# Projections beside the forgetting attention: staged in two alternating sets of tiles, stored from POOL's queue

## The chip, the cores and the metric

The kernel runs on one core of one Trainium2 chip. The metric is the device time of one execution in microseconds (us). Before the change it was 2829.44 us, the median of three runs (2826.55 to 2829.99). The engines are PE (matrix multiply; PEld is its weight load), DVE (vector), ACT (scalar and activation), POOL (GpSimd) and SP (SyncE, which here only issues DMAs). Every engine works through its own instructions in a fixed order.

## The reference

The program is two transformer blocks on 1024 tokens of width 1024. The first (a hybrid of attention and convolution, and a mixture of experts) is not touched. The second has a recurrent branch (HGRN, 8 heads) and a forgetting attention ("fox", 16 heads of 64), followed by an output projection. What matters here is the second branch and the projections that feed it:

```python
u = rmsnorm_2(h, norm_w[i])
proj = jnp.einsum('bsd,de->bse', u, w_in[i])
hq, hf, hi, hg, fq, fk, fv, fg, fz = jnp.split(proj, SPLIT_POINTS, axis=-1)
y_h = hgrn2_branch(hq, hf, hi, lb_all[i], hgrn_gn[i]) * jax.nn.silu(hg)
y_f = fox_branch(fq, fk, fv, fz, fox_fb[i]) * jax.nn.silu(fg)
...
# fox_branch, one block of 128 queries
logits = (jnp.einsum('bhtd,bhsd->bhts', qb, kb).astype(f32) * scale
          + F[:, :, q0:q1, None] - F[:, :, None, :q1])
probs = jax.nn.softmax(jnp.where(mask, logits, -jnp.inf), axis=-1)
outs.append(jnp.einsum('bhts,bhsd->bhtd', probs.astype(v.dtype), vb))
```

## The kernel before

All products are made from numbers that are split into a high and a low part (three matrix products for one). `u` stays in SBUF as `uh`, `ul`. A **job** is one block of weight columns (`wk` loads it into `raw`, ACT writes `whi`, DVE writes `wlo`), and a job has several **units**; one unit makes a 128x512 piece of the projection in PSUM (`mm`) with 24 matrix products of 512 columns, or 48 of 256.

`fox_jobs(pr)` lists the jobs for a pair of heads. There are three kinds of unit: `value` (V, for every second pair, four units), `qk` (Q and K, two units each) and `gate` (two units). A unit of the first two kinds calls `staged`: ACT writes the high part into the tile `sth`, DVE writes the low part into `stl`, and both are stored to DRAM tensors (`V2_d`, `Q2_d`, `K2_d`). A `gate` unit works in `sth` alone (four ACT and two DVE instructions) and stores to `G2_d`. The profile drops the digit and shows these tensors as V_d, Q_d, K_d, G_d. Both tiles lie in the pool `pj` with `SB = 1`, that is one buffer each: the next unit's ACT write to `sth` waits until the store of the unit before it has landed, and its DVE write to `stl` likewise. The stores are issued by SP (lines 1166, 1173, 1181), two DMAs for each part of V, one for the others: 144 DMAs in all, 128 to 256 KB each. SP also issues all loads of this stage, in one order with the stores: the weights (`raw`, line 835) and, for each head, `K`, `Q`, `V`, `nF` and for each pair `gs` (lines 1268 to 1280).

The units of pair 0 (ten of them) run inside the last HGRN head, the other 54 beside the attention. `fox()` goes over 128 steps (16 heads by 8 query blocks). `fox_scores` runs two steps ahead: PE makes `sc`, DVE makes `lg` (from `nF` and the tile `Gd`), ACT takes the exponential. `fox_values` transposes `lg` on PE (`tp`), ACT and DVE split it into `pT`, and PE multiplies it with V (`av`). Units are due at one in about 1.93 steps (`FPROJ / left` = 104 / 54). After step 104 come the weights and first parts of the output projection (`out_load`, `out_part`).

POOL's queue holds in this stage: `Gd` (line 1277, once a head), the clearing of `pT` (1318), and the stores of `yT_d` (line 76, from `self.store`). The final order on each engine is set by a scheduler that simulates the program, not by the text alone.

Of the kernel before, what the change touches and what calls it, by code (L numbers as in the profile page):

```python
# [8 lines left out]
F32 = mybir.dt.float32  # L9
F32R = mybir.dt.float32r  # L10
# [9 lines left out]
P = 128  # L20
# [7 lines left out]
EPS = 1e-6  # L28
NE = 16
CAP = 128  # L30
SB = 1
LOOK = 1
NCV = 31
NR = 6
# [6 lines left out]
def f(ap):  # L41
    return ap.bitcast(F32)
# [7 lines left out]
class Kernel:  # L50
# [729 lines left out]
    def block2(self):  # L780
        with ExitStack() as st:
            self.stu = ExitStack()
            up = self.pool(self.stu, "uT", side="right")
            self.u = [(self.t(up, [P, KB, 512], F32R, f"uh{g}"), self.t(up, [P, KB, 512], F32R, f"ul{g}")) for g in range(2)]
            self.pj = self.pool(st, "pj")
            self.jobs, self.ready = [], []
            with ExitStack() as st2:
                self.pp = self.pool(st2, "b2p", 2, space=PSUM)
                self.ffn_out()
                self.hgrn()  # L790
            self.fox()
# [353 lines left out]

    def fox_jobs(self, pr):

        nc, w = self.nc, self.pj

        def staged(ps, scale=None):  # L1150
            hi = self.t(w, [P, 512], F32R, "sth", bufs=SB)
            lo = self.t(w, [P, 512], F32R, "stl", bufs=SB)
            if scale is None:
                self.split(ps, hi, lo)
            else:
                nc.scalar.activation(hi, ps, AF.Copy, scale=scale)
                nc.vector.scalar_tensor_tensor(lo, ps, scale, f(hi), op0=ALU.mult, op1=ALU.subtract)
            return hi, lo

        def value(b):  # L1160
            def go(ws):
                ps = self.toks(ws, b)
                parts = staged(ps.rearrange("p b c -> p (b c)"))
                for j, part in enumerate(parts):
                    for k in range(2):
                        nc.sync.dma_start(self.V2_d[j, (b + k) * P:(b + k + 1) * P, pr * P:pr * P + 256], f(part[:, k * 256:(k + 1) * 256]))
            return go

        def qk(dst, scale, g):
            def go(ws):  # L1170
                parts = staged(self.chan(ws, g), scale)
                for j, part in enumerate(parts):
                    nc.sync.dma_start(dst[pr, j, :, g * 512:(g + 1) * 512], f(part))
            return go

        def gate(g):
            def go(ws):
                ps = self.chan(ws, g)
                e = self.sigmoid(w, ps, "sth", SB)
                nc.vector.tensor_tensor(e, e, ps, op=ALU.mult)  # L1180
                nc.sync.dma_start(self.G2_d[pr, :, g * 512:(g + 1) * 512], e)
            return go
        if pr % 2 == 0:
            self.job(6144 + pr * P, 256, [value(b) for b in range(0, 8, 2)])
        self.job(4096 + pr * P, P, [qk(self.Q2_d, -0.125, g) for g in range(2)])
        self.job(5120 + pr * P, P, [qk(self.K2_d, None, g) for g in range(2)])
        self.job(7168 + pr * P, P, [gate(g) for g in range(2)])

    def fox(self):
        nc, I = self.nc, self.I  # L1190
        with ExitStack() as st:
            w = self.w = self.pool(st, "fx")
            pp = self.pp = self.pool(st, "fxp", 2, space=PSUM)
            self.nmm = 2
            self.cmask = self.t(w, [P, P], F32, "cmask")
            nc.sync.dma_start(self.cmask, I["k_cmask"])
            for pr in range(1, 8):
                self.fox_jobs(pr)
            units = [(h, tb) for h in range(16) for tb in range(8)]
            left = len(self.ready) + sum(len(j[2]) for j in self.jobs)  # L1200
            due = [((j - 3) * FPROJ / left, self.fill) for j in range(left)]
            due += [(x, lambda q=q: self.out_load(q)) for q, x in enumerate(FLOAD)]
            due += [(FK0 + j * (len(units) - FK0) / 8, lambda j=j: self.out_part(0, j)) for j in range(8)]
            due.sort(key=lambda x: x[0])
            self.X = {}
            LOOK = self.LOOK
            for i in range(LOOK):
                self.fox_scores(*units[i])
            for i, u in enumerate(units):
                if i + LOOK < len(units):  # L1210
                    self.fox_scores(*units[i + LOOK])
                while due and due[0][0] <= i:
                    due.pop(0)[1]()
                self.fox_values(*u)
            for tb in range(2):
                self.out_part(1, tb)
# [15 lines left out]
    def out_part(self, half, tb):  # L1232

        nc, w = self.nc, self.pj
        t = slice(tb * P, (tb + 1) * P)
        y = self.y_half(w, half, tb, ("raw", "whi", "wlo"), (2, 3))
        h = self.t(w, [P, 512], F32, "sth", bufs=SB)
        nc.sync.dma_start(h, self.h2_d[t, 0:512])
        ps = self.t(self.pp, [P, 512], F32, "mm", bufs=self.nmm)
        wo = [self.wo[0, half * 2 + q] for q in range(2)]  # L1240
        self.mm3(ps, [(y[k], (wo[k // 4][0][:, k % 4, :], wo[k // 4][1][:, k % 4, :])) for k in range(KB)])
        nc.vector.tensor_tensor(h, h, ps, op=ALU.add)
        self.store(self.h2_d[t, 0:512], h)
# [291 lines left out]
```

## Time and profile before

| | |
|---|---|
| median of 3 runs | 2829.44 us |
| the profiled execution | 2830.79 us |
| its span, first to last instruction | 2828.9 us |
| PE busy | 2636.2 us, 93% |
| last HGRN stage, 1390 to 1890 us | PE busy 498.46 of 500 us |
| attention with projections, 1890 to 2450 us | PE busy 523.12 of 560 us |

The profile covers one execution. Its span leaves 1.9 us outside, and the execution is 1.35 us over the median. Times in the rows are counted from the span's start. A "busy" PE is one that has a matrix product under way; the granted clock (PEclk) is 1.00 at 2.4 GHz and 0.50 at 1.2 GHz.

### The profile page before, as it was taken

What the parts mean: (1) busy time and instruction counts of PE and PEld (TensorE: products, weight loads), DVE (VectorE), ACT (ScalarE), POOL (GpSimd) and SP (SyncE); (2) the same over time, 40 slices, a digit from 0 to 9 for tenths busy, and PEclk for the clock granted to TensorE, in tenths of its full rate; (3) what the DMA queues carried; (4) which work ended last, traced back from release to release, by engine and by line L of the source; (5) the groups of instructions that cost most, each with busy time, mean ns of one, the idle gap of its engine ahead of it and who ended that gap; (6) DMA issues with size and microseconds to landing.
All of it is one profiled execution on the core that took longest, in us unless ns stands there. A gap on an engine that the chain in (4) does not pass through costs nothing.

```text
span 2828.9 us, 38725 instructions
## 1 busy us (share of the span) xinstructions
PE 2636.2 (93%) x14237; PEld 2216.2 (78%) x14237; DVE 1998.8 (71%) x3298; ACT 1620.6 (57%) x2858; POOL 250.1 (9%) x355
## 2 busy tenths in 40 slices
PE   8999999898799999997799999998999998989998
PEld 5777888787588877775689999997878787777786
DVE  6965899845698888885656767763777676785535
ACT  4213898734477777775644555543665665674335
POOL 0101000001300000000100000000111110231000
PEclk9999999999899999999799999999999999999999
DMA  7666332245699999997512122336665667465612
GB/s 302 203 236 211 90 96 90 91 160 198 241 390 381 363 377 370 375 359 239 218 39 46 46 46 38 49 79 171 168 168 136 161 156 144 143 186 200 195 60 82
DMA packets 306018, 516.44 MB, mean 183 GB/s; under 512 B 52529, under 2 KB 180094, under 8 KB 304804
## 3 DMA queue, kind: packets, MB, share of 16 engines
q1 hardware_dynamic: 288556, 456.04, 51.0%
q0 software_dynamic: 11136, 36.25, 4.3%
q10 hardware_dynamic: 6136, 21.67, 2.0%
q8 instruction: 113, 1.85, 0.3%
q14 instruction: 77, 0.63, 0.1%
HBM read 421.01 MB, written 92.88 MB: 182 GB/s over the span
## 4 chain that ended last, share of the span: by engine, by line
PE 72%; DMA 10%; ACT 7%; DVE 6%; issue 3%; SPq 1%; POOL 0%; DVEq 0%; ACTq 0%; POOLq 0%
PE mm L82 13%; PE mm L84 13%; PE mm L83 12%; PE av L1333 2%; PE pu L763 2%; PE pu L764 2%; PE pu L762 2%; PE pg L763 2%; PE py L764 2%; PE py L763 2%; PE py L762 2%; PE pg L764 2%; PE sc L1052 2%; PE pg L762 2%; PE tp L1324 1%
## 5 line engine op out<-in xcount | busy, mean ns | idle before, releaser
L88 DVE TENSOR_TENSOR wlo<-raw,whi 128x2048 fp32r<-128x2048 f32 (+1 forms) x280 | 541.9, 1962 | 172.2 <-ACT whi L87 168.1
L87 ACT CAST whi<-raw 128x2048 fp32r<-128x2048 f32 (+1 forms) x284 | 459.8, 1656 | 136.5 <-PE mm L83 62.1
L82 PE MATMUL mm<-uh,whi 128*128 128x512 f32 x640 | 257.4, 402 | 0.9 <-ACT uh L824 0.9
L83 PE MATMUL mm<-ul,whi 128*128 128x512 f32 x640 | 254.1, 397 | 0.0
L84 PE MATMUL mm<-uh,wlo 128*128 128x512 f32 x640 | 253.8, 397 | 0.0
L84 PE MATMUL mm<-whi,ul 128*128 128x256 f32 x768 | 220.9, 288 | 0.0
L82 PE MATMUL mm<-whi,uh 128*128 128x256 f32 x768 | 220.6, 287 | 0.0
L83 PE MATMUL mm<-wlo,uh 128*128 128x256 f32 x768 | 218.2, 284 | 0.0
L82 PEld LDWEIGHTS mm<-whi,uh 128*128 128x128 f32 x768 | 147.4, 192 | 0.2
L84 PEld LDWEIGHTS mm<-whi,ul 128*128 128x128 f32 x768 | 147.5, 192 | 0.1
L83 PEld LDWEIGHTS mm<-wlo,uh 128*128 128x128 f32 x768 | 147.2, 192 | 0.2
L1302 ACT ACTIVATE lg<-lg,sm 128x128 f32<-128x128 f32 (+7 forms) x128 | 99.5, 777 | 82.2 <-DVE sm L1301 81.6
L84 PEld LDWEIGHTS mm<-uh,wlo 128*128 128x128 f32 x640 | 122.3, 191 | 24.4
L446 ACT ACTIVATE e<-sc,mx 128x512 f32<-128x512 f32 (+1 forms) x192 | 117.9, 624 | 40.3 <-DVE mx L445 39.5
L82 PEld LDWEIGHTS mm<-uh,whi 128*128 128x128 f32 x640 | 122.2, 191 | 22.9 <-ACT uh L824 1.4
L83 PEld LDWEIGHTS mm<-ul,whi 128*128 128x128 f32 x640 | 122.4, 191 | 21.7
L82 PE MATMUL mm<-xh,whi 128*128 128x512 f32 x320 | 127.2, 399 | 2.4 <-DVE stl L88 1.4
L1333 PE MATMUL av<-pT,V 128*128 128x256 f32 x640 | 109.9, 300 | 19.6 <-ACT pT L87 13.8
L83 PE MATMUL mm<-xl,whi 128*128 128x512 f32 x320 | 126.9, 398 | 0.0
L84 PE MATMUL mm<-xh,wlo 128*128 128x512 f32 x320 | 126.3, 396 | 0.5 <-DVE wlo L88 0.5
L1333 PEld LDWEIGHTS av<-pT,V 128*128 128x128 f32 x640 | 92.3, 196 | 43.0 <-ACT pT L87 30.5
L1298 DVE SCALAR_TENSOR_TENSOR lg<-sc,FT,nF 128x512 f32<-128x512 f32 (+3 forms) x160 | 91.6, 582 | 39.7 <-PE sc L1295 27.1
(392 smaller groups left out, 7006.2 us busy)
## 6 DMA issues: line engine op xcount, KB each, us to landing
raw<-in_w_gate_dram SPq DMA_DIRECT2D x64, 1024.0 KB
raw<-in_w_up_dram SPq DMA_DIRECT2D x64, 1024.0 KB
raw<-in_w_down_dram SPq DMA_DIRECT2D x64, 1024.0 KB
raw<-in_w_in_dram SPq DMA_DIRECT2D x76, 512.0 KB
wada<-in_w_ada_dram SPq DMA_DIRECT2D x32, 512.0 KB
Q<-Q_d SPq DMA_DIRECT2D x64, 256.0 KB
yraw<-yT_d SPq DMA_DIRECT2D x22, 512.0 KB
wa<-in_w_ada_dram SPq DMA_DIRECT2D x8, 1024.0 KB
```

Source lines behind the costliest of these rows:

```text
L82: self.nc.tensor.matmul(ps, ah, bh, start=(i == 0), stop=False)
L83: self.nc.tensor.matmul(ps, ah, bl, start=False, stop=False)
L84: self.nc.tensor.matmul(ps, al, bh, start=False, stop=(i == n - 1))
L87: self.nc.scalar.copy(hi, src)
L88: (eng or self.nc.vector).tensor_tensor(lo, src, f(hi), op=ALU.subtract)
L446: nc.scalar.activation(e[:, c0:c0 + n], ps[:, :n], AF.Exp, scale=-1.0, bias=mx[:, m, c:c + 1], accum_out=sm[:, m, c:c + 1])
L762: self.nc.tensor.matmul(ps[n], xh[:, i, :], hi[:, k, c], start=(i == 0), stop=False)
L763: self.nc.tensor.matmul(ps[n], xh[:, i, :], lo[:, k, c], start=False, stop=False)
L764: self.nc.tensor.matmul(ps[n], xl[:, i, :], hi[:, k, c], start=False, stop=(i == KB - 1))
L1298: nc.vector.scalar_tensor_tensor(lg[:, c0:c0 + full], ps[:, :full], Ft, nF[:, c0:c0 + full], op0=ALU.subtract, op1=ALU.add)
L1302: nc.scalar.activation(lg[:, :n], lg[:, :n], AF.Exp, scale=-1.0, bias=sm[:, 0:1], accum_out=sm[:, 1:2])
L1333: nc.tensor.matmul(ps[:, :256], V[:, k, :], pT[k // 4][j][:, k % 4, :], start=(k + j == 0), stop=(k == nkb - 1 and j == 1))
```

## The change

Inside `fox()`, a second set of `sth` and `stl` is made in the pool `fx`, and units take the two sets in turn. During the last HGRN head there is still only the set in `pj`. All 144 stores go through `self.store`, that is through POOL's queue in place of SP's. `SB` is gone; the tiles that used it keep one buffer in their pool. `out_part` keeps its `sth` in `pj`.

```diff
@@ class Kernel, block2
             self.jobs, self.ready = [], []
+            self.staging, self.turn = [self.pj], 0
...
@@ fox_jobs
-        nc, w = self.nc, self.pj
+        nc = self.nc
+
+        def place():
+
+            self.turn = (self.turn + 1) % len(self.staging)
+            return self.staging[self.turn]
 
         def staged(ps, scale=None):
-            hi = self.t(w, [P, 512], F32R, "sth", bufs=SB)
-            lo = self.t(w, [P, 512], F32R, "stl", bufs=SB)
+            w = place()
+            hi = self.t(w, [P, 512], F32R, "sth", bufs=1)
+            lo = self.t(w, [P, 512], F32R, "stl", bufs=1)
...
-                        nc.sync.dma_start(self.V2_d[j, (b + k) * P:(b + k + 1) * P, pr * P:pr * P + 256], f(part[:, k * 256:(k + 1) * 256]))
+                        self.store(self.V2_d[j, (b + k) * P:(b + k + 1) * P, pr * P:pr * P + 256], f(part[:, k * 256:(k + 1) * 256]))
...
-                    nc.sync.dma_start(dst[pr, j, :, g * 512:(g + 1) * 512], f(part))
+                    self.store(dst[pr, j, :, g * 512:(g + 1) * 512], f(part))
...
-                e = self.sigmoid(w, ps, "sth", SB)
+                e = self.sigmoid(place(), ps, "sth", 1)
                 nc.vector.tensor_tensor(e, e, ps, op=ALU.mult)
-                nc.sync.dma_start(self.G2_d[pr, :, g * 512:(g + 1) * 512], e)
+                self.store(self.G2_d[pr, :, g * 512:(g + 1) * 512], e)
...
@@ fox
             self.nmm = 2
+            self.staging = [self.pj, w]
```

The line numbers of the changed kernel are 1 lower up to `block2`, 6 higher in `fox_jobs` and 7 higher behind it. PE, ACT, DVE, POOL and SP do the same work as before; 144 DMA issues move from SP to POOL, and the scheduler sets some neighbours in another order.

ACT where the attention begins. `mm_16755`, `mm_16792` and `mm_16823` are the first three units of pair 1 (Q, Q, K), `lg_16718` is the first query block of head 0. Before:

```order
L1156 ACTIVATE sth_16780<-mm_16755 128x512
L87 CAST whi_17035<-raw_17033 128x1024
L1302 ACTIVATE lg_16718,sm_16701<-lg_16718,sm_16701 128x128
L1156 ACTIVATE sth_16817<-mm_16792 128x512
L1304 ACTIVATE lg_16718<-lg_16718,sm_16701 128x128
L1302 ACTIVATE lg_16727,sm_16728<-lg_16727,sm_16728 128x256
```

and now:

```order
L1162 ACTIVATE sth_16780<-mm_16755 128x512
L86 CAST whi_17035<-raw_17033 128x1024
L1162 ACTIVATE sth_16817<-mm_16792 128x512
L86 CAST sth_16848<-mm_16823 128x512
L1309 ACTIVATE lg_16718,sm_16701<-lg_16718,sm_16701 128x128
L1311 ACTIVATE lg_16718<-lg_16718,sm_16701 128x128
```

The second and third unit's high parts now stand ahead of the first exponential of head 0.

PE at the same place. `mm_16823` is the third unit, `mm_16860` the fourth, `sc_16901` the scores of a later query block of head 0, which need a PSUM buffer that DVE frees with `lg`. Before:

```order
L82 MATMUL mm_16823<-uh_2157_11155,whi_16788 128x512
L83 MATMUL mm_16823<-ul_2158_11156,whi_16788 128x512
L84 MATMUL mm_16823<-uh_2157_11155,wlo_16789 128x512
L1295 MATMUL sc_16901<-K_16702,Q_2927_16699 128x512
L1295 MATMUL sc_16901<-K_16702,Q_2928_16700 128x512
```

and now:

```order
L83 MATMUL mm_16823<-uh_2157_11155,wlo_16789 128x512
L81 MATMUL mm_16860<-uh_2159_11157,whi_16788 128x512
...
L83 MATMUL mm_16860<-uh_2159_11157,wlo_16789 128x512
L1331 MATMUL tp_16895<-ident_59,lg_16718 128x128
L1302 MATMUL sc_16901<-K_16702,Q_2927_16699 128x512
L1302 MATMUL sc_16901<-K_16702,Q_2928_16700 128x512
```

All 24 products of the fourth unit now stand ahead of these scores.

POOL at the same place: `Gd_16714` is head 0's. Before:

```order
L1318 MEMSET pT_3003_17080 128x128
L1318 MEMSET pT_3004_17081 128x128
L1277 TENSOR_TENSOR Gd_16714<-nF_16712,cmask_16697 128x1024
L76 DMA yT_d_85<-t_2972_16920 64x256
L1277 TENSOR_TENSOR Gd_17155<-nF_17153,cmask_16697 128x1024
```

and now:

```order
L75 DMA Q_d_88<-stl_16818 128x512
L75 DMA K_d_89<-sth_16848 128x512
L1284 TENSOR_TENSOR Gd_16714<-nF_16712,cmask_16697 128x1024
L75 DMA K_d_89<-stl_16849 128x512
L75 DMA K_d_89<-sth_16885 128x512
L75 DMA K_d_89<-stl_16886 128x512
L75 DMA yT_d_85<-t_2972_16920 64x256
L1284 TENSOR_TENSOR Gd_17155<-nF_17153,cmask_16697 128x1024
```

Head 0's `Gd` now stands behind the stores of the first two units and of the third unit's high part.

## Rows read from the trace of the kernel before

**Rows 1.** The page's first part: busy time, share of the span and number of instructions of each engine.

```profile
PE 2636.2 (93%) x14237; PEld 2216.2 (78%) x14237; DVE 1998.8 (71%) x3298; ACT 1620.6 (57%) x2858; POOL 250.1 (9%) x355
```

**Rows 2.** Busy time of each engine in a stretch: from:to and its length, then PE, PEld, DVE, ACT, POOL (with their instructions), the granted clock, the share of the DMA engines and GB/s. First the last HGRN stage, then the stage of the change.

```profile
1390.00:1890.00 500.00, 498.46 (x3487) 458.47 (x3486) 346.54 (x692) 254.92 (x514) 7.49 (x11) 1.00 0.25 50
1890.00:2450.00 560.00, 523.12 (x3018) 448.77 (x3018) 373.94 (x793) 324.89 (x649) 76.59 (x161) 0.98 0.62 155
```

**Rows 3.** Who waited for whom, PE alone, 1910 to 2440 us: total us, times, longest.

```profile
PE av L1333 <- ACT pT L87: 11.0, 7, 2.6
PE tp L1324 <- DVE pT L88: 10.3, 6, 6.1
PE av L1333 <- DVE pT L88: 4.1, 3, 3.2
PE sc L1295 <- DVE lg L1298: 3.1, 1, 3.1
PE sc L1295 <- DVE lg L1300: 2.8, 1, 2.8
PE tp L1139 <- DVE t L1133: 2.6, 1, 2.6
PE sc L1105 <- DVE ST L1058: 2.1, 1, 2.1
PE tp L1324 <- DVE lg L1300: 0.3, 1, 0.3
```

**Rows 4.** The chain that ended last, in order of time (start, length, what), around the longest idle time of PE in this stage; the first and the last row are the first and the last link through a staged store.

```profile
1893.30 8.43 DMA V_d<-sth
...
2337.65 0.61 DVE stl L88
2339.04 13.49 DMA V_d<-stl
...
2353.28 0.69 DVE pT L88
...
2380.84 9.42 DMA K_d<-sth
```

**Rows 5.** PE's timeline, the first instruction behind that idle time (start, length; in brackets the idle time before it and what ended it).

```profile
2354.10 1.51 PE L1324 MATMUL tp<-ident,lg 128*128 128x128 f32 x6 [6.06 <-DVE pT L88]
```

**Rows 6.** ACT's timeline, the `sth` writes of two neighbouring units at that place.

```profile
2336.37 0.57 ACT L87 CAST sth<-mm 128x512 fp32r<-128x512 f32 x1
2344.84 0.58 ACT L1156 ACTIVATE sth<-mm 128x512 fp32r<-128x512 f32 x1
```

**Rows 7.** SP's timeline there: a weight load, and behind it the two stores of the low part of V (start, time that the issues took).

```profile
2337.86 0.40 SPq L835 DMA_DIRECT2D raw<-in_w_in_dram  x1
2338.67 4.55 SPq L1166 DMA_DIRECT2D V_d<-stl  x2
```

**Rows 8.** What POOL's queue stores already in the kernel before: the instructions on POOL (ns shortest/median/longest), of `yT_d` beside the attention and of `h_d` behind it (the same 128x512 shape as Q, K and the gate); then, for `yT_d` between 1955 and 2440 us, the time from issue to landing in us; last the issue row of `h_d<-sth` (KB each, median us to landing).

```profile
L76 POOL DMA_DIRECT2D yT_d<-t x54: 521/529/552, 1976.2 to 2498.7; - x54
L76 POOL DMA_DIRECT2D h_d<-sth x10: 544/573/585, 2496.4 to 2591.5; - x10
...
DMA to landing us min/median/max: 1.9/4.1/11.6
...
h_d<-sth POOLq DMA_DIRECT2D x10, 256.0 KB, 2.5
```

**Rows 9.** Stretches as in rows 2: five that lie right behind idle times of PE.

```profile
1963.50:1966.80 3.30, 3.30 (x10) 2.69 (x10) 2.75 (x8) 3.04 (x9) 0.00 (x0) 0.50 0.70 227
2038.60:2041.90 3.30, 3.30 (x13) 3.01 (x14) 2.31 (x7) 1.80 (x5) 0.00 (x0) 0.50 1.00 277
2154.90:2158.00 3.10, 3.08 (x14) 3.08 (x15) 1.47 (x7) 2.55 (x6) 0.37 (x2) 0.50 0.59 215
2216.10:2219.40 3.30, 3.30 (x11) 2.82 (x12) 2.77 (x7) 1.19 (x3) 0.00 (x0) 0.50 0.22 86
2354.10:2359.30 5.20, 5.20 (x16) 4.41 (x17) 3.76 (x10) 2.92 (x7) 0.00 (x0) 0.50 0.66 71
```

**Rows 10.** Two stretches of the attention with no idle time of PE of any length.

```profile
1966.90:2036.30 69.40, 69.32 (x458) 61.91 (x457) 49.87 (x104) 43.91 (x85) 10.52 (x21) 1.00 0.67 175
2106.00:2151.00 45.00, 44.96 (x273) 39.25 (x272) 36.54 (x74) 29.74 (x59) 6.78 (x16) 1.00 0.64 161
```

**Rows 11.** The beginning of the attention on three timelines: PE's wait, head 0's `Gd` on POOL, and ACT's `sth` writes of the first and second unit of pair 1.

```profile
1961.55 1.50 PE L1295 MATMUL sc<-K,Q 128*128 128x512 f32 x4 [2.83 <-DVE lg L1300]
1958.78 2.33 POOL L1277 TENSOR_TENSOR Gd<-nF,cmask 128x1024 f32<-128x1024 f32 x1 [17.61 <-DMA nF<-F_d]
1947.04 0.60 ACT L1156 ACTIVATE sth<-mm 128x512 fp32r<-128x512 f32 x1 [5.68 <-PE mm L84]
1962.43 0.58 ACT L1156 ACTIVATE sth<-mm 128x512 fp32r<-128x512 f32 x1
```

**Rows 12.** The last HGRN head: DVE's longest wait for a staged store there, and PE's wait that follows from it.

```profile
1918.91 0.69 DVE L88 TENSOR_TENSOR stl<-mm,sth 128x512 fp32r<-128x512 f32 x1 [8.09 <-DMA Q_d<-stl]
1920.57 0.91 PE L1105 MATMUL sc<-V,t 128*128 128x128 f32 x6 [2.13 <-DVE ST L1058]
```

**Rows 13.** Head 1's `Gd` on POOL's timeline, its first reader on DVE's, and who waited for a `Gd` between 1890 and 2500 us (DVE alone; total, times).

```profile
1982.08 2.40 POOL L1277 TENSOR_TENSOR Gd<-nF,cmask 128x1024 f32<-128x1024 f32 x1 [5.38 <-DMA nF<-F_d]
1994.41 0.34 DVE L1300 SCALAR_TENSOR_TENSOR lg<-sc,FT,Gd 128x128 f32<-128x128 f32 x1
...
DVE lg L1300: 6.6, 1
```

More of the change, by code (lines that the diff above doesn't have):

```diff
@@ L30 @@
 CAP = 128
-SB = 1
 LOOK = 1
@@ L1236, in out_part @@
         y = self.y_half(w, half, tb, ("raw", "whi", "wlo"), (2, 3))
-        h = self.t(w, [P, 512], F32, "sth", bufs=SB)
+        h = self.t(w, [P, 512], F32, "sth", bufs=1)
         nc.sync.dma_start(h, self.h2_d[t, 0:512])
```

## The prediction

> **What bounds the kernel now.** I read the busy times first. PE is busy for 93% of the span [rows 1], but the average hides two kinds of stage. In the last HGRN stage PE is busy for 498.46 of 500 us; in the stage of the change it is busy for 523.12 of 560 us, so 36.9 us are idle, while DVE (374 us) and ACT (325 us) have room [rows 2]. PE is therefore the bound of this stage, and what can be won is its idle time and what its clock loses behind it. No speed-up of another engine counts unless it ends one of PE's waits.
>
> Next, what ends PE's waits. In the attention PE waits for `pT` or `lg` from ACT and DVE [rows 3]; neither row names a store. The chain of waits shows what made them late [rows 4]: DVE wrote the low part of a V unit at 2337.65; its store needed from 2339.04 to 2352.5 to land; only then could DVE write the next unit's `stl`, and behind that write, in DVE's fixed order, stood the `pT` that PE's transposes needed. PE idled for 6.06 us [rows 5]. Sixteen links through a staged store lie in the chain from 1893 to 2390 us, the first with 8.43 us, the last with 9.42, the longest this one [rows 4]. Most of each is hidden by products PE still has; the rest is rows 3. The next unit's `sth` came 8.47 us after this one's [rows 6], so with one set a store that takes longer than about 7 us stalls ACT or DVE, and many do.
>
> Why a store takes so long: SP's issue of those two stores took 4.55 us, directly behind a weight load [rows 7].
>
> **The change part by part.** *The second set.* A set is written again after two units, 16.9 us by rows 6, instead of 8.47 us. Of this ACT's write (0.58 us), DVE's (0.69 us, as in rows 12) and one issue on POOL (0.57 us, rows 8) take 1.84 us, so a store may need 15.1 us to land. The slowest link of the chain is 13.49 us; POOL's own stores beside the attention landed within 1.9 to 11.6 us [rows 8]. Both fit. So I take the waits on staged stores as gone in the attention, even without the other queue.
>
> *The queue.* 144 issues of 0.57 us (the `h_d<-sth` row, same shape as Q and K; the smaller `yT_d` rows lie at 0.53) are 82 us more on POOL, which is busy for 76.6 of 560 us [rows 2, 8]. All of it lies beside PE's work. It would cost something only where POOL's order makes a store late. I set POOL's new order against the times at which the kernel before produced the same tiles: by that estimate the median store is issued without any delay and the latest 5.7 us late. With POOL's median landing of 4.1 us that is far inside 15.1 us; only with the slowest, 11.6, would that one store be 2.2 us too late. On SP, 144 issues go, and the weight loads and the heads' loads no longer stand behind stores that wait for ACT or DVE. They become due earlier, but rows 3 show no PE wait on them, so I count nothing for that.
>
> A rule of the Trainium skill speaks against this half of the change: "DMA: Bandwidth & Descriptors", section "Issuing engines are not separate DMA queues", says that DMAs of all issuing engines run interleaved on the same 16 DMA engines and that another issuing engine saves only issue time. Rows 8 agree in part, since a 64 KB store from POOL can take 11.6 us. By that rule alone the forecast would lose the 2.1 us of the last HGRN head below and be otherwise the same.
>
> *The sum, PE's idle time.* In rows 3 the waits that lead back to staged stores are 11.0 + 10.3 + 4.1 + 3.1 + 2.1 = 30.6 us. Of them 2.1 us lie in the last HGRN head [rows 12], where there is still one set: there the only help is the other queue. That gain lies between 0 (POOL's slowest landing of 11.6 us is longer than the 8.09 us wait) and 2.1 us (POOL's median of 2.5 us for this shape); I take half, 1.0 us, so 29.5 us.
>
> *The beginning of the attention.* PE waits 2.8 + 0.3 us for `lg`, which waits for head 0's `Gd` [rows 3, 11]. The new order acts in both ways. `Gd` now stands behind the store of the third unit's high part. PE ended that unit at about 1958.7 (1961.55 less 2.83); ACT's 0.6 and POOL's 0.57 us put `Gd` at about 1959.9 instead of 1958.78, ending at 1962.2. But PE now has the fourth unit in front of the scores: 24 products, 5.8 us at the pace of the units before it (the first ended at 1947.0, the third at 1958.7), so it is busy until 1964.5. In rows 11 the wait ended 0.4 us after `Gd`; now that is 1962.6, inside the cover. The transpose that now stands ahead of the scores needs the finished `lg`, so I leave 0.2 us and take 2.9 of the 3.1 us, with 0 (the late `Gd` eats it) as the other end.
>
> *The clock.* Five stretches right behind these waits run at a granted clock of 0.50, that is 1.2 instead of 2.4 GHz: 3.3 + 3.3 + 3.1 + 3.3 + 5.2 = 18.2 us [rows 9]. The undisturbed stretches between them run at 1.00 [rows 10]. PE did in 18.2 us what takes 9.1 us at full clock. Before each of the five stood one of the waits that go, so 9.1 us go too; if the waits only shrink, some stretches may stay.
>
> *What is late next.* Where no store interferes, PE has idle time of 0.08 us in 69.4 and 0.04 in 45 us [rows 10], so the softmax chain does not become the bound at once. At this rate some 0.6 us come up new in 490 us. The 2.6 us in front of `tp` of the last HGRN head [rows 3] do not hang on a store and stay, as does everything behind 2450 us.
>
> Sum: 29.5 + 2.9 + 9.1 - 0.6 = 40.9 us. The profiled execution of 2830.79 would become 2789.9; it lies 1.35 us over the median, so I forecast a median of 2788.5, rounded to **2789 us**. At most: all 36.9 us of idle time and as much of half clock (9.1 and 1.7 more for the stretch behind the 2.6 us) make 47.7 us, that is 2782 as a median; 5 us more for loads that no longer queue behind stores give 2777 as the edge.
>
> **The rivals.** *The attention's own chain is next late.* For it: ACT and DVE still make `pT` just in time, and PE's order was chosen by a simulation with other times; once PE runs 7% faster through the stage, a part of the waits of rows 3 on `pT` can come back. Against it: rows 10. Price: if half of the 30.6 us and half of the 9.1 us stay, the gain is 21 us, 2808 us; with a quarter to three quarters 2799 to 2818.
>
> *The stores are no longer late but nothing moves.* For it: PE's waits name `pT` and `lg`, not stores, and a wait for several things is put down to the one that came last. Then the gain is under 5 us, 2825 to 2832. Against it: the chain links store, `stl`, `pT` and `tp` without a gap [rows 4, 5].
>
> *POOL makes `Gd` late: slower.* `Gd` now shares POOL's order with 118 stores beside the attention, each of which waits for ACT or DVE. Today only head 0's `Gd` is waited for [rows 13]; it costs PE 3.1 us and 1.65 us of half clock, 4.8 us. If that happened to the 13 heads whose projections run beside them, 62 us would come on top: 2830 - 42 + 62 = 2850; from nine heads on the kernel is slower than before. It decides from the point at which POOL is held up for longer than `Gd` leads its reader. Head 1's was done at 1984.5 [rows 13], 10 us ahead of its first reader at 1994.4. Against it: a delay of at most 5.7 us in the order as laid out above. A cause that would do the same is named by the Trainium skill, "SBUF — State Buffer", section "SBUF: two separate sides": certain DVE operations lock GpSimd out, so that DMAs issued from POOL wait for their descriptors, 3.1 us against 0.62 in its example; an estimate from that page would be 2.5 us more for each of 144 stores, 360 us on POOL. Rows 8 do not agree: 64 issues beside a DVE that is busy for two thirds of the time took 0.521 to 0.585 us.
>
> **How the numbers follow.** Forecast 0.76 (2777 to 2799), the attention's chain 0.13 (2799 to 2818), nothing moves 0.06, slower 0.05. A measurement of this kernel tells about 0.2% (5.7 us) from no change; the first two are beyond it, so faster 0.89, same 0.06, slower 0.05. The range takes in the forecast and the first half of the second case, 2777 to 2809: 0.76 and some 0.07.
>
> **What would show it.** In the profile of the changed kernel no wait of ACT `sth` or DVE `stl` on a DMA between 1950 and 2440 us; PE idle in that stage down from 37 to below 8 us; no stretch at 0.50 between the beginning of the attention and the last projection; `yT_d` and the new stores on POOL at 0.52 to 0.6 us each, landing within 12 us; one `Gd` at most that is waited for. I am wrong if PE waits for `pT` as long as before with no store in the chain (first rival), if the stores still stand in it, or if `lg` waits for `Gd` in several heads.

## The result, and the profile after

The changed kernel takes 2797.11 us, the median of four runs (2795.80 to 2800.15); the kernel before, run beside it, 2827.99 (2825.51 to 2829.99). The ratio is 0.9884 (95% interval 0.9865 to 0.9903), a gain of 30.9 us where 40.4 were forecast. The profiled execution took 2800.15 us, with a span of 2798.4.

Where the time came from is read best between marks, instructions that stand at the same place in both programs: the last transposes of the HGRN heads (1938.95 us before, 1936.51 after) and the first scores behind the last projection (2463.45 and 2432.26). First the three stretches of the kernel before, in the columns of [rows 2]:

```profile
1890.00:1938.95 48.95, 44.21 (x242) 37.79 (x242) 22.49 (x44) 20.26 (x46) 0.00 (x0) 1.00 0.41 102
1938.95:2463.45 524.50, 488.13 (x2823) 418.32 (x2823) 362.27 (x773) 315.06 (x626) 80.15 (x166) 0.98 0.63 157
2463.45:2828.90 365.45, 334.32 (x1581) 273.77 (x1581) 208.72 (x341) 181.94 (x315) 39.66 (x61) 0.96 0.47 148
```

and the same three of the changed kernel:

```profile
1890.00:1936.51 46.51, 43.69 (x238) 37.26 (x237) 22.45 (x43) 19.63 (x46) 7.02 (x13) 1.00 0.42 108
1936.51:2432.26 495.75, 477.84 (x2823) 411.41 (x2824) 362.41 (x773) 315.10 (x626) 144.73 (x285) 0.99 0.66 166
2432.26:2798.40 366.14, 335.67 (x1581) 275.70 (x1581) 208.46 (x341) 182.02 (x315) 39.86 (x61) 0.95 0.47 148
```

In the middle stretch PE has the same 2823 products. It is 28.75 us shorter: PE's idle time fell from 36.37 to 17.91 us (18.46), and the products themselves took 10.29 us less; fewer of them ran at half clock (granted clock 0.98 before, 0.99 after). The HGRN head gave 2.44 us, and the rest of the program lost 0.69. DVE's and ACT's work is the same to 0.2 us.

Who waited for whom, PE alone, 1910 to 2440 us, which answers to [rows 3]:

```profile
PE av L1340 <- ACT pT L86: 10.5, 7, 7.3
PE sc L1302 <- DVE lg L1307: 3.3, 1, 3.3
PE tp L1139 <- DVE t L1133: 2.6, 1, 2.6
PE sc L1302 <- DMA Q<-Q_d: 1.4, 1, 1.4
PE tp L1331 <- DVE pT L87: 1.2, 2, 0.8
PE av L1340 <- DVE t L1346: 0.7, 1, 0.7
PE tp L1331 <- ACT lg L1311: 0.7, 1, 0.7
PE av L1340 <- DVE pT L87: 0.5, 1, 0.5
PE sc L1105 <- DVE ST L1058: 0.2, 1, 0.2
```

The 3.3 us lie behind the last projection and were there before, at 2463 us, as were the 2.6. Of the rest one wait stands out, 7.3 us. ACT and DVE waited as follows for staged stores, and for one `Gd`, in the same stretch; of the first row 7.7 us, and the fourth, lie in the last HGRN head, where there is one set:

```profile
DVE stl L87 <- DMA Q_d<-stl: 9.2, 2, 7.7
ACT sth L883 <- DMA K_d<-sth: 8.7, 1, 8.7
DVE lg L1307 <- POOL Gd L1284: 2.7, 1, 2.7
DVE stl L87 <- DMA K_d<-stl: 0.7, 1, 0.7
ACT sth L86 <- DMA Q_d<-sth: 0.5, 1, 0.5
```

So one long wait for a staged store is left beside the attention, ACT's 8.7 us, at a gate unit. The timelines of SP, ACT, POOL and PE show how it became PE's (start, length; in brackets the idle time before and what ended it):

```profile
2330.77 2.72 SPq L1282 DMA_DIRECT2D nF<-F_d  x1
2331.63 0.59 ACT L86 CAST sth<-mm 128x512 fp32r<-128x512 f32 x1 [0.26 <-PE mm L83]
2342.35 0.59 ACT L86 CAST sth<-mm 128x512 fp32r<-128x512 f32 x1 [0.50 <-DMA Q_d<-sth]
2345.55 2.39 POOL L1284 TENSOR_TENSOR Gd<-nF,cmask 128x1024 f32<-128x1024 f32 x1 [16.76 <-DMA nF<-F_d]
2347.90 0.58 POOL L75 DMA_DIRECT2D K_d<-sth  x1
2350.05 0.39 PE L83 MATMUL mm<-uh,wlo 128*128 128x512 f32 x1
2350.12 0.57 POOL L75 DMA_DIRECT2D K_d<-sth  x1
2357.87 0.60 ACT L883 ACTIVATE sth<-mm 128x512 f32<-128x512 f32 x1 [8.71 <-DMA K_d<-sth]
2361.95 0.58 PE L1340 MATMUL av<-pT,V 128*128 128x256 f32 x1 [7.29 <-ACT pT L86]
```

and the chain that ended last shows how long the store took to land:

```profile
2347.90 9.89 DMA K_d<-sth
```

The two `sth` writes belong to a pair's first and second K unit, and the two issues on POOL, in the same order, are their stores. The gate unit behind them takes the set of the first K unit, since the two sets alternate. ACT had finished that unit's high part at 2332.22. On POOL its store stood behind a `Gd` that waited for its load `nF`, so it was issued 15.68 us later, and it then needed 9.89 us to land: 25.6 us in all. The gate's last product ended at 2350.4 (PE's L83 at 2350.05), so the set was wanted 18.2 us after 2332.22. Behind the gate's write, in ACT's order, stood the `pT` for which PE waited, begun at 2361.33.

### The profile page after: what moved, and what is told of

Read it like the earlier page. It is cut to its first block, busy times and chain, and to the rows that moved or that the text cites. A ratio compares the mean times of both kernels' runs of the same rounds, so it can differ in the third digit from the quotient of the medians.

```text
span 2798.4 us, 38785 instructions
## 1 busy us (share of the span) xinstructions
PE 2624.4 (94%) x14237; PEld 2209.1 (79%) x14237; DVE 1998.6 (71%) x3298; ACT 1621.3 (58%) x2858; POOL 328.6 (12%) x499
## 4 chain that ended last, share of the span: by engine, by line
PE 77%; DMA 7%; ACT 6%; DVE 6%; issue 3%; POOL 1%; SPq 0%; DVEq 0%; POOLq 0%; ACTq 0%
PE mm L81 14%; PE mm L82 14%; PE mm L83 13%; PE av L1340 3%; PE pu L762 2%; PE pu L763 2%; PE pu L761 2%; PE pg L762 2%; PE py L763 2%; PE py L762 2%; PE py L761 2%; PE pg L763 2%; PE tp L1331 2%; PE sc L1052 2%; PE sc L1302 2%
## 5 line engine op out<-in xcount | busy, mean ns | idle before, releaser
L83 PE MATMUL mm<-uh,wlo 128*128 128x512 f32 x640 | 251.6, 393 | 0.0
L83 PE MATMUL mm<-whi,ul 128*128 128x256 f32 x768 | 220.4, 287 | 0.0
L83 PEld LDWEIGHTS mm<-whi,ul 128*128 128x128 f32 x768 | 147.1, 192 | 0.1
L83 PEld LDWEIGHTS mm<-uh,wlo 128*128 128x128 f32 x640 | 120.7, 189 | 23.9
L83 PE MATMUL mm<-xh,wlo 128*128 128x512 f32 x320 | 126.5, 397 | 0.5 <-DVE wlo L87 0.5
L444 DVE TENSOR_REDUCE mx<-sc 128x1 f32<-128x512 f32 (+1 forms) x192 | 110.1, 593 | 7.6 <-PE sc L443 6.7
```

What stands on the lines that cost most here:

```text
L83: self.nc.tensor.matmul(ps, al, bh, start=False, stop=(i == n - 1))
L444: nc.vector.tensor_reduce(mx[:, m, c:c + 1], ps[:, :n], axis=AX.X, op=ALU.min)
```

## The experiments

Theory: PE's waits came from tiles written again before their stores had landed; the second set removes them, and the changed kernel falls short by the one store that is still too late. Rivals: POOL's queue does the work; the attention's own chain of ACT and DVE is what PE now waits for.

Ratios are to the kernel before in runs on the same chip. E1 to E8 ran on one chip, E9 to E11 on another, E12 and E13 on a third. The scheduler orders each kernel anew, so some neighbours on PE differ from run to run. The expectations of E4, E6, E7 and E12 give the late K store 15.5 us, some 4.9 of them ahead of its issue. They reckon from the write of the second K unit (2342.35). The store is the first K unit's, as the result shows: 15.7 us until its issue and 9.9 us of landing, against 18.2.

**E1, two sets, SP's queue.** Against the changed kernel, all three kinds of unit:

```diff
-                    self.store(dst[pr, j, :, g * 512:(g + 1) * 512], f(part))
+                    nc.sync.dma_start(dst[pr, j, :, g * 512:(g + 1) * 512], f(part))
```

> Two sets as in the changed kernel, but all 144 stores on SP's queue again. Theory (the second set does the work, since a store may then take 15.1 us and SP's slowest took 13.49): 2790 to 2803 us, no ACT sth or DVE stl wait on a DMA of more than 2 us inside the attention, and the one in the last HGRN head back at 8 us. Rival (the queue does the work: SP's stores stand behind loads and hold loads back): over 2812 us, with such waits left. The scheduler sets some PE instructions in another order (186 lines of difference), so a few us either way say nothing.

Measured: 2797.48 us, ratio 0.9859 (0.9842 to 0.9875): the time is the theory's. Two waits are longer than its 2 us, ACT's of 3.5 and DVE's of 4.8 us for stores of Q, since SP's longest store took 17.7 us; the one in the last HGRN head is 9.9 us. PE is busy for 464.55 of the 470 us from 1940 to 2410 (the same stretch of the changed kernel has 456.53), and no idle time over 3.2 us is left there.

**E2, one set, POOL's queue.** Against the changed kernel:

```diff
-            self.staging = [self.pj, w]
```

> One set as in the kernel before, all 144 stores on POOL's queue. Theory (the second set does the work): a store of 4 to 9 us (POOL's medians by tile in the changed kernel) against a slack of about 7 us still stalls ACT and DVE often: 2812 to 2830 us, PE waits of over 15 us in the attention. Rival (the queue does the work): 2803 us or less. Second rival (with one set each wait for a landing now holds POOL's order too, and Gd stands in it): over 2835 us.

Measured: 2869.41 us, ratio 1.0116 (1.0095 to 1.0136). The queue alone is not worth nothing: it costs 32 us. The price came out as the second rival had it, but by the theory's way, not by `Gd`: in E2 DVE waits only 2.1 us for a `Gd`, and no store beside the attention was issued more than 3.0 us after its tile was ready, while the waits for staged stores have more than doubled. The theory's own 2812 to 2830 us was too low. ACT's longest and DVE's, 1940 to 2420 us:

```profile
ACT sth L1162 <- DMA V_d<-sth: 17.1, 3, 8.4
ACT sth L86 <- DMA Q_d<-sth: 16.4, 2, 9.0
ACT sth L1162 <- DMA Q_d<-sth: 12.2, 3, 6.5
...
DVE stl L87 <- DMA Q_d<-stl: 12.3, 2, 9.3
DVE stl L1163 <- DMA V_d<-stl: 9.4, 2, 4.8
```

The table sets kernels side by side. The waits are the sums of ACT `sth` and DVE `stl` for staged stores, 1940 to 2420 us. The landings are worked out from the semaphore events of each trace, from the start of an issue to the last event of that DMA (a few events are missing for SP's). How long a store stood on its queue is worked out from the program's order and the same trace.

```
kernel                  waits for stores   stores: number, median,   Q loads:  nF loads:  time against
                        ACT     DVE        over 7 us, longest        median    median     before
before (one set, SP)    24.0    23.3       113   3.3   22   17.7     5.8       5.8        1
E2 one set, POOL        72.0    35.4       105   6.0   41   16.8     9.4      10.3        1.0116
E8 one set, ACT         26.1    42.1       107   4.7   33   16.4     6.4       5.9        1.0114
E1 two sets, SP          3.5     4.8       118   4.8   28   17.7     7.0       7.4        0.9859
E5 two sets, POOL        9.8     1.2       118   6.6   55   15.3     9.1      10.3        0.9873
E6 three sets, POOL      0       0         118   6.0   54   15.5     8.9      10.3        0.9845
E9 three sets, SP        0       0         118   4.8   27   17.7     6.9       6.7        0.9836
```

With one set a store has about 7 us [rows 6]; on SP 22 stores took longer, on POOL 41. The mechanism is that of the prediction, with POOL's queue on the wrong side of it.

**E8, one set, ACT's queue.** As E2, with `nc.scalar.dma_start`.

> One set as before, all 144 stores on ACT's queue. With one set on POOL's queue the stores' landing rose from a median of 3.3 to 6.0 us and the head's Q loads from 5.8 to 9.4. Theory A (that comes from taking the stores out of SP's order: loads and stores are now under way together): median landing of 5 us or more here too, Q loads at 8 us or more, 2845 to 2875 us. Theory B (it is POOL's own way of storing): landing 3 to 4 us, Q loads at 6 us, 2838 us or less plus what ACT loses by 144 issues.

Measured: 2868.31 us, ratio 1.0114 (1.0100 to 1.0129). The time is theory A's, the landings lie between the two: 4.7 us for stores, 6.4 for Q loads. So part of the longer landing came with ACT's queue too, when the stores no longer stood in one order with the loads; the rest, above all the loads' 9.4 us, only with POOL's. How much of each is in E2's 32 us stays open, since ACT also pays for the issues here.

**E5, the changed kernel again**, on the chip of E1 and E2.

> The changed kernel itself, as a measure for the other runs. Theory (the second set brings the gain, and POOL's queue costs some of it, because stores that no longer stand in one order with the loads land later: median 5.6 us against 4.8 from SP with two sets): ratio to the kernel before 0.988 to 0.991, above the 0.986 of two sets with SP's queue. Rival (the queue makes no difference): 0.985 to 0.987.

Measured: 2799.98 us, ratio 0.9873 (0.9859 to 0.9887). The ratio lies between the two ranges, and its interval overlaps that of E1: a cost of the queue with two sets is not shown. The late K store is there again (15.3 us behind `Gd`, 10.8 us of landing), with 8.1 us of idle time of PE.

**E6, three sets, POOL's queue.** A third set alone did not fit (E3, which gave no time): a set takes 4 KB per partition, and 1.5 were free. Here the room comes from `gs`.

```diff
-            self.staging = [self.pj, w]
+            self.staging = [self.pj, w, self.pool(st, "fy")]
...
+            self.gs = self.t(w, [P, SEQ], F32, "gs", bufs=1)
...
-            if i == 0:
-                gs = self.t(w, [P, SEQ], F32, "gs", bufs=2)
-                nc.sync.dma_start(gs, self.G2_d[pr])
-                X["gs", pr] = gs
+            X["gs", pr] = self.gs
+            nc.sync.dma_start(self.gs[rows, :], self.G2_d[pr, rows, :])
```

> Three sets in turn, stores on POOL; the room comes from gs, which is now one tile whose halves are loaded head by head (two loads of 256 KB for one of 512). Theory (what the changed kernel falls short is a store that took 15.5 us against a slack of 15.1): with three sets the slack is some 23 us, no idle time of PE of over 2 us between 1970 and 2400 us, ratio 0.003 below the changed kernel's. Rival (ACT and DVE are late there for another reason): an idle time of over 4 us left near 2355, ratio the same.

Measured: 2789.84 us, ratio 0.9845 (0.9833 to 0.9858), 10.1 us less than E5. POOL still holds the K store back for 15.4 us (it waits 16.48 us for `nF` there), and it lands 10.5 us after its issue, but that is 2.8 us before its set is written again: nobody waits for a store. PE's waits, 1940 to 2420 us:

```profile
PE av L1339 <- ACT pT L86: 3.1, 6, 1.3
PE tp L1330 <- DVE pT L87: 1.5, 1, 1.5
PE sc L1301 <- DMA Q<-Q_d: 1.3, 1, 1.3
PE tp L1330 <- ACT lg L1310: 1.1, 1, 1.1
```

That is what the attention's own chain asks for when no store is late: 7.0 us in these rows.

**E10, the control of E6**: `gs` as in E6, two sets.

> The control of three sets: the changed kernel (two sets, POOL) with gs as one tile loaded by halves, and no third set. Theory (the third set, not gs, took away the late store): ratio within 0.0015 of the changed kernel's 0.9873, idle time of over 4 us left near 2355. Rival (the smaller gs loads do it): 0.984 to 0.985.

Measured: 2800.06 us, ratio 0.9870 (0.9849 to 0.9891), with 8.54 us of idle time at 2363. The K store again stood 15.1 us behind `Gd`. The third set did it, not `gs`.

**E9, three sets, SP's queue.** E6 with the line of E1.

> Three sets in turn (room from gs as in the run of three sets on POOL), all 144 stores on SP's queue. Theory (with a slack of some 23 us no store is late from either queue, so the queue no longer matters): within 0.002 of the 0.9845 of three sets on POOL. Rival (loads that land at 9 us from the side of POOL's stores, against 6 to 7 with SP's, cost PE something of their own): ratio 0.981 to 0.983.

Measured: 2787.39 us, ratio 0.9836 (0.9814 to 0.9858), the lowest ratio of all runs, but not to be told from E6. Where nobody waits for a store, no effect of the queue on the time can be told. SP's order, too, holds a store back here, a K store for 14.6 us, without harm. PE's waits, 1940 to 2420 us (the 3.3 us are those behind the last projection):

```profile
PE sc L1301 <- DVE lg L1306: 3.3, 1, 3.3
PE tp L1330 <- DVE pT L87: 2.3, 2, 1.8
PE av L1339 <- ACT pT L86: 1.2, 4, 0.4
PE av L1339 <- DVE t L1345: 0.7, 1, 0.7
```

**E11, a second `sth` only, SP's queue.** E1 with

```diff
-            lo = self.t(w, [P, 512], F32R, "stl", bufs=1)
+            lo = self.t(self.pj, [P, 512], F32R, "stl", bufs=1)
```

> A second tile for the high part alone (sth in turn, one stl), all stores on SP's queue. In the kernel before ACT waits 24 us and DVE 23 us for staged stores between 1940 and 2420. Theory A (each wait counts where it stands): ACT's waits for stores go, DVE's 20 to 30 us stay, about half of the 40 us gain of two sets on SP: 2812 to 2825 us where before is 2837, ratio 0.991 to 0.996. Theory B (the two parts go in lockstep, so the one that is left takes over): ratio 0.997 or more, and DVE's waits grow to over 40 us.

Measured: 2820.98 us, ratio 0.9949 (0.9929 to 0.9969). ACT's 24.0 us are gone, DVE's stay at 23.5 (23.3 before): theory A. The ratio lies in its range, with about a third of E1's gain (0.0051 of 0.0141). Each tile's waits count where they stand, though not for the half that theory A named.

**E4, E7 and E12, three tries at the late store itself.** E4 issues `nF` ahead of its head's K, Q and V:

```diff
+            nF = self.t(w, [P, SEQ], F32, "nF", bufs=2)
+            nc.sync.dma_start(nF, rowbc(self.F_d[h:h + 1, :]))
             for half in range(2):
                 hr = slice(half * 64, (half + 1) * 64)
...
-            nF = self.t(w, [P, SEQ], F32, "nF", bufs=2)
-            nc.sync.dma_start(nF, rowbc(self.F_d[h:h + 1, :]))
```

> The changed kernel with each head's nF load issued ahead of its K, Q and V loads, so that Gd on POOL, and the stores queued behind it, need not wait for the V loads. Of the 15.5 us of the late K store, 4.9 lie ahead of its issue (Gd waits for nF and runs 2.4 us) and 9.9 behind it. Theory A (POOL's order made it late): idle time at 2362 us down from 7.3 to 2.5 us or less, 2788 to 2794 us. Theory B (landing under the load of the loads made it late): the idle time stays at 5 us or more, 2794 to 2800 us.

E7 makes `Gd` on DVE (`nc.vector.tensor_tensor(Gd, ...)`):

> The changed kernel with Gd made by DVE, so that no store on POOL stands behind a Gd that waits for its load. Theory A (POOL's order is a main part of the late K store, 4.9 of 15.5 us): the idle time near 2362 us goes, ratio 0.002 to 0.004 below the changed kernel's, unless DVE now waits for nF. Theory B (slow landing alone): it stays, the same ratio. If DVE waits for nF ahead of pT, PE waits longer: ratio above 0.992.

E12 loads the next head's `nF` at the head's fourth query block (the call alone is shown):

```diff
+        if tb == 3 and h < 15:
+            self.nF_load(h + 1)
```

> The changed kernel (two sets, POOL) with nF of the next head loaded in the middle of the head before it, so that no Gd on POOL waits for a load of its own head. Of the 15.5 us that the late K store took, 4.95 lay behind such a Gd. Theory (POOL's order and slow landing both belong to it): Gd's waits for nF go from 67 to below 15 us, ACT's wait for that store from 8.7 to about 3.8 us, PE's idle time near 2362 from 7.3 to 2 to 3 us, ratio 0.9845 to 0.9865. Rival (landing alone decides): an idle time of over 6 us stays, ratio as the changed kernel's 0.9873 or above.

Measured: E4 2811.15 us, 0.9909 (0.9894 to 0.9924); E7 2839.15, 1.0010 (1.0000 to 1.0019); E12 2809.69, 0.9923 (0.9906 to 0.9940). All three are slower than the changed kernel, and no theory of E4 or E12 foresaw why. In both, `nF` was issued earlier, and `Gd` could start 26.0 and 26.5 us after the `sth` write of the pair's first Q unit, instead of 29.7. But the scheduler also moved `Gd` forward on POOL, ahead of the stores of the second Q unit, so that POOL came to it 2.9 us after that write instead of 12.9. So POOL waits longer, not shorter, and holds up more stores. From 1910 to 2440 us all waits of `Gd` for `nF` sum to 105 us in either (66.8 in the changed kernel). E4's ACT (the second Q unit), POOL and PE:

```profile
2336.53 0.59 ACT L1162 ACTIVATE sth<-mm 128x512 fp32r<-128x512 f32 x1
2352.57 2.35 POOL L1284 TENSOR_TENSOR Gd<-nF,cmask 128x1024 f32<-128x1024 f32 x1 [23.09 <-DMA nF<-F_d]
2355.56 0.57 POOL L75 DMA_DIRECT2D Q_d<-sth  x1
2366.51 0.58 PE L1340 MATMUL av<-pT,V 128*128 128x256 f32 x1 [13.13 <-ACT pT L86]
```

The store that ACT then waits for stood 15.7 us on POOL in the changed kernel, 15.3 in E5 and 15.1 in E10, and PE's idle time was 7.3, 8.1 and 8.5 us; it stood 18.4 us in E4 and 18.9 in E12, with 13.1 and 12.2 us. In E7, with `Gd` off POOL, no store beside the attention stood there for more than 2.4 us, this K store for 0.3, and neither ACT nor DVE waited for one. So the store's delay on POOL comes from `Gd`. What the time would be with that alone mended no run shows, since in E7 DVE takes over the wait for `nF`, ahead of `pT`, a case that its expectation names. DVE's and then PE's waits there, 1940 to 2420 us:

```profile
DVE Gd L1284 <- DMA nF<-F_d: 41.7, 7, 14.4
...
PE av L1340 <- ACT pT L86: 22.1, 6, 6.0
PE av L1340 <- DVE pT L87: 13.4, 1, 13.4
```

**E13**, E9 with E12's edit:

> Three sets on SP with the same earlier nF. Theory (there no wait on a store or a Gd is left that PE feels, but for 3.3 us of lg behind a Gd at 2419): within 0.0015 of the 0.9836 of three sets on SP, at best 0.982. Rival (nF ahead of its head takes DMA time from the weights): 0.986 or more.

Measured: 2801.22 us, ratio 0.9896 (0.9878 to 0.9914), above E9's. The ratio is the rival's, but E9 ran on another chip, and whether DMA time of the weights is the cause was not looked into further.

## Why the prediction was right, and where not

- *PE is the bound, its waits lead back to staged stores.* Right. The waits of ACT and DVE for stores fell from 47.3 us to some 11, and with three sets to none. Of the signs that were named, four did not come: ACT waited 8.7 us for a store, PE's idle time in the middle stretch is 17.91 us and not below 8, one stretch at 0.50 is left, and stores took up to 15.6 us, not 12, to land.
- *Waits that lead back to stores: 28.5 us in the projection stretch (29.5 less the HGRN head), and 2.9 at the beginning of the attention, less 0.6.* The stretch gave 18.46 us of idle time, not 30.8. Of the 12.3 missing, 7.3 are the one late store, and about 2 lie at the beginning, where PE now waits 1.4 us for `Q` and 0.7 for `lg`. The others are short waits for `pT`: the step that put all 25.4 us of them down to stores was too generous, since E6 keeps 4.6 us with no store late. That is the first rival, on a small scale.
- *Half clock, 9.1 us.* Right in cause and near in size: the products took 10.29 us less. The parts differ. One stretch like the five of [rows 9] came again, that behind the late store, and the one behind the 2.6 us of the HGRN head, which the sum left standing, went (the granted clock is 1.00 from 1386 to 2359 us), as these stretches of the changed kernel show (the granted clock stands behind the engines' times):

```profile
1940.00:2354.60 414.60, 408.42 (x2455) 353.58 (x2453) 305.12 (x648) 261.22 (x518) 123.76 (x246) 1.00 0.69 171
2361.95:2365.80 3.85, 3.85 (x14) 3.46 (x15) 1.65 (x4) 2.47 (x5) 0.72 (x3) 0.50 1.04 219
```

- *The last HGRN head, 1.0 us between 0 and 2.1.* PE's wait fell by 1.9 us. It is not the queue's doing for certain: with the same staging and POOL's queue E2 has 4.9 us there, E5 0.6, and with SP's queue E1 has 4.5, E9 2.6.
- *A store may take 15.1 us; POOL's take at most 11.6, with a delay of at most 5.7, and moving the queue costs nothing.* **This is the step that failed**, in its delay. 5.7 us is what the kernel before gives for this very store, from the end of the K unit's high part (2370.03) to the end of the `Gd` that now stands ahead of the store (2375.72):

```profile
2366.44 0.55 SPq L1275 DMA_DIRECT2D nF<-F_d  x1
2369.45 0.58 ACT L87 CAST sth<-mm 128x512 fp32r<-128x512 f32 x1 [0.67 <-PE tp L1324]
2373.33 2.39 POOL L1277 TENSOR_TENSOR Gd<-nF,cmask 128x1024 f32<-128x1024 f32 x1 [9.46 <-DMA nF<-F_d]
```

  In the changed kernel it is 15.68 us. `Gd` could start 14.8 us after the issue of `nF` instead of 6.9 (in E1, with SP's queue, 8.1), and the K unit's high part ended 1.4 us after that issue instead of 3.6. Loads land later beside POOL's stores: the median `nF` load takes 10.3 us in all three such kernels of the table, 5.8 to 7.4 us with SP's queue. Of the 118 stores beside the attention four were issued more than 5.7 us late, all behind this `Gd`; that only one of them was wanted soon is luck. With the delay of 5.7 us the landing of 9.89 us would have fitted into the 18.2. The price as read from the trace is 7.29 us of idle time and half of the 3.85 us at half clock, 9.2 us; E6 puts it at 10.1. The profiled span falls short of the forecast by 10.4 us, with smaller differences either way in the other terms.
- *The landings.* They were too low as well. I took POOL's from small stores that had the queue for themselves: with 118 stores on it the median is 5.6 us, the longest 15.6. SP's 13.49 was the slowest of the chain alone; outside it the kernel before has one of 17.7 us. In E1 that left ACT and DVE 8.3 us of waits, with 3.2 us as PE's longest.
- *POOL makes `Gd` late.* Not so: one `lg` waited for one `Gd`, 2.7 us. The harm went the other way: `Gd`, waiting for its load, made a store late.

By the Trainium skill ("DMA: Bandwidth & Descriptors", section "Issuing engines are not separate DMA queues") another issuing engine saves only issue time. The runs lie nearer to that than to my term: another issuing engine brought no gain that can be measured with two or three sets, and with one it cost 1.1%. The prediction has the forecast lose 2.1 us by that rule; the sum holds only 1.0 us to lose. That the new queue slows stores and loads alike, 3.3 to 6.0 and 5.8 to 9.4 us, goes beyond what the prediction drew from it. The lock on descriptors of which the Trainium skill speaks in "SBUF — State Buffer", section "SBUF: two separate sides", estimated in the prediction at 360 us, did not show: the 144 issues on POOL took 0.539 to 0.583 us.

## What to carry to other kernels

When an engine waits to overwrite a staging tile, compare the time between two writes with the whole distribution of the store's landing, its queue's delay added, and buy buffers until the slowest fits: one, two and three sets gave 1, 0.986 and 0.984 on the same queue. Do not take a landing time from a queue that is nearly empty, and do not expect a second queue to be free; here loads and stores that stood in one order disturbed each other less. In a fixed order, look for the instruction that waits for a load ahead of the store, and do not time it by the kernel before: the change can make that load land later and the store be ready sooner.

## What was not expected of the hardware

- Taking 144 stores out of SP's order raised the landing of the Q loads that stayed on SP from a median of 5.8 to 9.4 us with POOL's queue, 6.4 with ACT's (one set each).
- POOL's stores are made of fewer, larger DMA packets: from 1940 to 2420 us the changed kernel's POOL queue shows 9328 packets for 27.47 MB, 6704 of 4 KB and 2624 end marks of 4 bytes. ACT's queue in E8 stores the same tiles in packets of 2 KB and, for V, 1 KB. Whether this is why POOL's land later was not tried.
- In E4 an `nF` load took 22.4 us to land (median in the changed kernel 10.3), although it was issued ahead of most of its head's K and Q loads. It landed 1.1 us ahead of the Q load issued behind it and 2.5 us behind the K load issued before it, which had itself taken 22.2 us; two weight loads of 512 KB had been issued in the 11.3 us before `nF`. To issue a load ahead of its neighbours saved little here, since the loads issued before it still landed first.
